# Attention layers of a hybrid backbone: order of the head preparation, token sums of squares, and the engine of the split differences

## Chip, cores, metric

One core of a Trainium2 chip runs the whole program. The metric is the device time of one execution in microseconds (us). A median is given with the runs it comes from; the profile is one execution with its own time.

## The reference, cut to what matters

Two layers work on 256 context and 256 latent tokens of width 1024. Each layer has a mixer and a sparse expert block.

```python
xr, ckv, kr, gk, gv, rg, cq, gq, mg = split_cols(h @ w_in, KV_SIZES + Q_SIZES)
kv = rms_norm(ckv, g_kv) @ w_ukv          # MLA: 8 heads, latent of 128
q  = rms_norm(cq, g_q) @ w_uq             # query latent of 256
t  = rms_norm(heads(gq or gk), g)         # GQA: per-head norm over 64
p  = softmax(q @ k.T * scale);  o = p @ v # latent tokens read 512 keys, context 256
out = sum(sigmoid(mg[k]) * (y[k] @ w_branch[k]) for k in (lru, mla, gqa)) @ w_out
```

Every `rms_norm` needs a sum of squares per token. In layer 0 all 512 tokens have queries (two query blocks per pair of heads); in layer 1 only the 256 latent ones (one block).

## The kernel before, in words

Activations stand with channels on partitions and tokens along the row. Large projections are made of three passes in the fast matmul format: weight and input are each split into a rounded part (hi) and the difference (lo), and hi\*hi, hi\*lo and lo\*hi are summed. `split` (L238) makes hi on ScalarE (L240) and lo either on VectorE (L242) or, when an engine is handed in, on GpSimd through `gtt` (L247). `wsplit` (L252) does it for a weight in tiles of 4 blocks of 128 rows; these tiles have 3 buffers (tag `sp`). `dense` (L262) is the three passes and `proj` (L409) a whole projection, which splits on VectorE. Matmuls in plain float32 count as two instructions in the trace.

`mixer` (L414) runs in this order. The recurrent input is projected and convolved. `lru(0)` and `lru(1)` (L488) work out the recurrence: matmuls, a chain of tanh and exp on ScalarE, one square root over a tile `lt` that has a single buffer, then products and scans on VectorE, with one product per direction and the sum `yr` on GpSimd. Between them the latents are projected: `ckv` (L556), the 32 columns `kr` (L565), `cq` (L572). Their squares are summed by a matmul with 32 columns of ones into rows (L561, L575), copied to SBUF (L563, L576) and turned to tokens by `tok_major` (L533), after which `rsqrt` (L153) runs one start and three rounds of three small dependent VectorE instructions. `gates` (L594) projects the gate of the recurrent branch, and `y0` (L611) is the product, split in hi and lo.

Then come MLA (branch 1) and GQA (branch 2) attention. Work that has nothing to do with the attention under way is laid between its steps: `fill` is a `Queue` (L73) of steps of the branch before. `merge` (L625) gives three steps for each of 8 column blocks j: `load_gate`/`gate0`, `split_gate`/`gate1`, `load_branch`/`branch`. Each first part (load and split) is issued one step before its matmuls. The modulation steps are put in the same queue. So the queue holds 37 steps for the MLA of layer 0 (24 merge, 13 modulation), 32 for its GQA, 25 and 24 in layer 1. TensorE keeps the program order from L814 on (`pin`); the other engines are ordered by the framework's scheduler.

`attend` (L728) walks over units (a pair of heads i and a query block). Per unit: `turn` (L710) turns a block of the softmax and ScalarE copies it out of the only `t` buffer, `scores` of the next unit, `values`. `fill.spread(gaps)` spreads what is left in the queue evenly over the gaps, 35 in layer 0 and 23 in layer 1; where there are fewer steps than gaps, some gaps get none, the first always. Before the attention, the steps that prepare the first pair of heads (`mla(0)`, L815: q_rope, turn_q, queries, keys, values; `gqa(0)`, L918: one) are issued with one fill step after each. The preparation of each later pair (`early`, L739 to L748) is issued during the last unit of the pair before, two steps after a turn, the rest at its end.

For GQA, `query` (L840) and `query_sums` (L849) are issued for four pairs, then the copy of the sums (L887), four `rope_in` (L888) with a fill step after every second, `tok_major` (L892), and `rsqrt` into `qrs` (L898), which every softmax of GQA multiplies (L682) before its exponential (L685).

Of the kernel before, what the change touches and what calls it, by code (L numbers as in the profile page):

```python
# [7 lines left out]
F32 = mybir.dt.float32  # L8
F32R = mybir.dt.float32r
BF16 = mybir.dt.bfloat16  # L10
I32 = mybir.dt.int32
AF = mybir.ActivationFunctionType
ALU = mybir.AluOpType
# [4 lines left out]
EPS = 1e-6  # L18
# [79 lines left out]
class Net:  # L98
# [307 lines left out]
            self.nc.vector.scalar_tensor_tensor(sc[:, :, r], sc[:, :, r], 1.0, g, op0=ALU.add, op1=ALU.mult)  # L406


    def proj(self, tag, w, c0, m, cs, hT, mark=None, xs=None):  # L409
        p = self.ps(tag)  # L410
        self.dense(p[:m, cs], self.wsplit(w, c0, 8, m), hT, xs or cs, mark=mark)
        return p

    def mixer(self, l, pb):  # L414
# [7 lines left out]
        t0 = lo // 128  # L422
# [17 lines left out]
        hT = []  # L440
# [89 lines left out]
            s.activation(q[:, cs], p[:, cs], AF.Square)  # L530
            return q

        def tok_major(rows, parts):  # L533

            pc = self.ps("t", (128, 4, 128))
            for t in range(4):
                n = parts(t)
                if n:
                    self.te.transpose(pc[:, t, :n], rows[:n, 128 * t:128 * t + 128], self.ident[:n, :n])
            return pc  # L540

        def rope_in(x, n, perm, cs, sn, eng):

# [11 lines left out]
        w = self.win(l, 512)  # L555
        p = self.proj("acc", w, 0, 128, A, hT, "ckv")  # L556
        ckv = self.gr("a", "ckv")
        q = sq_of(p, A)
        v.tensor_scalar(ckv, p, sm[:, SGKV:SGKV + 1], None, op0=ALU.mult)
        pa = self.ps("m")  # L560
        self.te.matmul(pa[0:32, :], self.ones32, q, start=True, stop=True)  # L561
        rows = self.sqp.tile([128, 512], F32, tag="rows", name="rows")
        v.tensor_copy(rows[:32, :], pa[:32, :])  # L563
        lru(0)
        p = self.proj("acc", w, 128, 32, A, hT)  # L565
        kr = self.gr("a", "kr")
        v.tensor_copy(kr[:32], p[:32])
        w = self.win(l, 1440)
        cq = [self.gl("a", "cq") for _ in range(2)]
        pa = self.ps("m")  # L570
        for i in range(2):
            p = self.proj("acc", w, 128 * i, 128, L, hT)  # L572
            q = sq_of(p, L)
            v.tensor_scalar(cq[i], p[:, L], self.gqs[l][:, i:i + 1], None, op0=ALU.mult)
            self.te.matmul(pa[32:64, L], self.ones32, q[:, L], start=i == 0, stop=i == 1)  # L575
        v.tensor_copy(rows[32:64, L], pa[32:64, L])  # L576
        rope_in(kr[:, 256:], 32, self.permM, self.cosM, self.sinM, v)
        pc = tok_major(rows, lambda t: 64 if t >= t0 else 32)
        ms = self.tiny([128, 4, 2], name="mms")
        v.memset(ms, 1.0)  # L580
        v.tensor_scalar(ms[:, :, 0:1], pc[:, :, 0:1], 1.0 / 128, EPS, op0=ALU.mult, op1=ALU.add)
        v.tensor_scalar(ms[:, t0:, 1:2], pc[:, t0:, 32:33], 1.0 / 256, EPS, op0=ALU.mult, op1=ALU.add)
        mrs = self.tiny([128, 4, 2], name="mrs")
        self.rsqrt(mrs, ms, [128, 4, 2])
        pb = self.ps("m")
# [8 lines left out]
        def gates(i2):  # L594
            w = self.win(l, 928 + 256 * i2)
            for i in (2 * i2, 2 * i2 + 1):
                p = self.proj("acc", w, 128 * (i % 2), 128, L, hT)
                a, x = self.gl("z", "ga"), self.gl("gt", "gx")
                s.activation(x, p[:, L], AF.Copy)
                s.activation(a, p[:, L], AF.Square, scale=0.044715 ** 0.5)  # L600
                v.scalar_tensor_tensor(a, a, 1.0, x, op0=ALU.add, op1=ALU.mult)
                s.activation(a, a, AF.Tanh, scale=0.7978845608028654)
                v.scalar_tensor_tensor(a, a, 1.0, x, op0=ALU.add, op1=ALU.mult)
                gel.append(a)
# [20 lines left out]
        def merge(b, j, y):  # L625

            c0 = 128 * (j % 2)

            def load_gate():
                if j % 2 == 0:  # L630
                    st["m"] = self.win(l, 2208 + 1024 * b + 128 * j)
                st[j, 0] = self.wsplit(st["m"][:, 0:4], c0, 4)
                st["m", j] = st["m"]

            def gate0():
                st["pm"] = self.ps("acc")
                self.dense(st["pm"][:, L], st.pop((j, 0)), hT[:4], L, last=False, mark=f"mg{b}.{j}")

            def split_gate():
                st[j, 1] = self.wsplit(st.pop(("m", j))[:, 4:8], c0, 4)  # L640

            def gate1():
                pm = st.pop("pm")
                self.dense(pm[:, L], st.pop((j, 1)), hT[4:], L, first=False)
                st["gt"] = gt = self.gl("gt", "gt")
                s.activation(gt, pm[:, L], AF.Tanh, scale=0.5)

            def load_branch():
                if j % 4 == 0:
                    st["b"] = self.wblock(ap["w_branch"][l, b, :, 512 * (j // 4):512 * (j // 4) + 512]  # L650
                                          .rearrange("(k p) c -> p k c", p=128), (4, 512))
                st[j, 2] = self.wsplit(st["b"], 128 * (j % 4), 4)

            def branch():
                gt, pp = st.pop("gt"), self.ps("acc")
                self.dense(pp[:, L], st.pop((j, 2)), y, Z)
                if b == 0:
                    zT[j] = self.gl("z", "zT")
                    v.scalar_tensor_tensor(zT[j], gt, 1.0, pp[:, L], op0=ALU.add, op1=ALU.mult)
                    return  # L660
                v.scalar_tensor_tensor(gt, gt, 1.0, pp[:, L], op0=ALU.add, op1=ALU.mult)  # L661
                self.gtt(zT[j], zT[j], gt, ALU.add)
                if b == 2:
                    hi, lw = self.gl("a", "zh", F32R), self.gl("a", "zl", F32R)
                    self.split(zT[j], hi, lw)
                    zs[j] = (hi, lw)

            return (load_gate, gate0), (split_gate, gate1), (load_branch, branch)
# [59 lines left out]
        def attend(units, early):  # L728
# [7 lines left out]
                    next(share)  # L736
            for n, u in enumerate(units):
                nxt = units[n + 1] if n + 1 < len(units) else None
                todo = list(early.pop(nxt.i, ())) if nxt and nxt.i != u.i else []  # L739
                for k, g_ in enumerate(u.groups):  # L740
                    u.turn(*g_)
                    if k < len(u.groups) - 1:
                        for f in todo[:2]:
                            f()
                        del todo[:2]
                        next(share)
                for f in todo:
                    f()  # L748
                if nxt:
                    nxt.scores(0)  # L750
                u.values()
                next(share)
                if nxt:
                    nxt.scores(1)
                next(share)
# [59 lines left out]
        for f in mla(0):  # L815
            f()
            fill()
        attend([Unit(i, st_, lambda i=i: [[(q[:96], k[:96])] for q, k in zip(QTs[i], KTs[i % 2])],
                     lambda c, hh, i=i: Vs[i][:, c, 64 * hh:64 * hh + 64], lambda t, hh: mrs[:, t, 1:2], y1)
                for i in range(4) for st_ in sts], {i: mla(i) for i in range(1, 4)})  # L820
# [9 lines left out]
        p = self.proj("acc", w, 128, 128, A, hT)  # L830
        gvT = self.gr("a", "gvT")
        s.activation(gvT, p, AF.Copy)
        pa = self.ps("m")
        self.te.matmul(pa[0:32, :], self.onesh, qk_, start=True, stop=True)
        rows = self.sqp.tile([128, 512], F32, tag="rows", name="rows")
        v.tensor_copy(rows[:32, :], pa[:32, :])
        gq, sqs = [], []
        pa = self.ps("o")

        def query(i):  # L840
            if i % 2 == 0:
# [5 lines left out]
            gq.append(x)  # L847

        def query_sums(i):  # L849
            self.te.matmul(pa[32 * i:32 * i + 32, L], self.onesh, sqs[i][:, L], start=True, stop=True)  # L850

        query(0)
        pc = tok_major(rows, lambda t: 32)
        ms = self.tiny([128, 4, 2], name="kms")
        v.tensor_scalar(ms, pc[:, :, 0:2], 1.0 / 64, EPS, op0=ALU.mult, op1=ALU.add)
        krs = self.tiny([128, 4, 2], name="krs")
# [26 lines left out]
        fill_branch(1, y1)  # L883
        fill(1)
        query_sums(3)
        rows = self.sqp.tile([128, 512], F32, tag="rows", name="rows")
        v.tensor_copy(rows[:, L], pa[:, L])  # L887
        for i in range(4):  # L888
            rope_in(gq[i][:, Tq - 256:], 128, self.permG, self.cosG, self.sinG, g)
            if i % 2 == 0:  # L890
                fill(1)
        pc = tok_major(rows, lambda t: 128 if t >= t0 else 0)  # L892
        ms = self.tiny([128, 4, 8], name="qms")
        v.tensor_scalar(ms[:, t0:].rearrange("p t (c r) -> p t c r", r=2),
                        pc[:, t0:, :].rearrange("p t (c r) -> p t c r", r=32)[:, :, :, 0:2],
                        1.0 / 64, EPS, op0=ALU.mult, op1=ALU.add)
        qrs = self.tiny([128, 4, 8], name="qrs")
        self.rsqrt(qrs[:, t0:], ms[:, t0:], [128, 4 - t0, 8])  # L898
        if l:
            for _ in self.fix:  # L900
                self.preload(l)
# [15 lines left out]

        for f in gqa(0):  # L918
            f()
            fill()  # L920
        attend([Unit(i, st_, lambda i=i: QK[i], lambda c, hh, i=i: gv[:, c, 64 * (i // 2):64 * (i // 2) + 64],
                     lambda t, hh, i=i: qrs[:, t, 2 * i + hh:2 * i + hh + 1], y2)
                for i in range(4) for st_ in sts], {i: gqa(i) for i in range(1, 4)})
# [850 lines left out]
```

## Time and profile before

| what | us |
|---|---|
| median of 3 runs (lowest, highest) | 1567.58 (1566.35, 1568.84) |
| the profiled execution, its own time | 1564.28 |
| span of its instructions | 1562.4 |
| TensorE matmul busy in the span | 1406.4 (90%) |
| VectorE, ScalarE, GpSimd busy | 845.8, 572.7, 183.5 |

The span runs: start and mixer of layer 0 to about 600, experts of layer 0 to 930, mixer of layer 1 to 1286, experts of layer 1 to the end. Busy shares are averages over these; what a mixer edit is worth is read from what TensorE waits for in the mixer's own stretches. The granted clock is given as a share of 2.4 GHz.

### The profile page before, as it was taken

The page shows a single profiled execution, that of the slowest core. Times are in us where ns is not written, and L with a number is a line of the kernel's source. Part 1 is how long each engine was busy: PE and PEld are TensorE (multiplying, and loading weights), DVE is VectorE, ACT ScalarE, POOL GpSimd, SP SyncE. Part 2 cuts the span into 40 slices and gives each one's busy share as a digit, 9 for nine tenths or more (in the row PEclk, how much of TensorE's full clock was granted, in tenths as well). Part 3 has the DMA queues.
Part 4 walks back from the last instruction along what each step waited for, and adds up shares of the span by engine and source line. Part 5 has one row for each costly group of instructions (what it writes and reads, how often), then busy time and mean ns, then how long its engine had stood idle before and what let it go on. Part 6 is the DMA issues. An engine that isn't in the chain of part 4 may idle for free. (4 is left out here: it accounts for less than half of the span.)

```text
span 1562.4 us, 19617 instructions
## 1 busy us (share of the span) xinstructions
PE 1406.4 (90%) x7313; PEld 877.1 (56%) x7313; DVE 845.8 (54%) x1963; ACT 572.7 (37%) x1122; POOL 183.5 (12%) x157
## 2 busy tenths in 40 slices
PE   6987899998989999699999969969979995999996
PEld 3645556666667776244444426656768992444433
DVE  4667545436654346745444456776476656444223
ACT  3455434433553342111111136635456551222212
POOL 0013200001101111200000010321010131000000
PEclk9999999999999999799999989979989997999998
DMA  9401323422313566799999823412232586999991
GB/s 357 160 28 53 135 108 108 145 71 81 135 55 133 197 263 259 270 420 419 414 409 392 330 99 108 162 54 73 90 108 82 189 325 240 419 419 419 419 417 50
DMA packets 61839, 336.56 MB, mean 215 GB/s; under 512 B 8864, under 2 KB 9376, under 8 KB 26272
## 3 DMA queue, kind: packets, MB, share of 16 engines
q1 hardware_dynamic: 55536, 324.20, 53.6%
q0 software_dynamic: 4608, 6.30, 1.2%
q10 hardware_dynamic: 1584, 4.64, 0.8%
q8 instruction: 62, 1.02, 0.3%
q14 instruction: 49, 0.40, 0.1%
HBM read 341.40 MB, written 4.19 MB: 221 GB/s over the span
## 5 line engine op out<-in xcount | busy, mean ns | idle before, releaser
L64 PE MATMUL ps_acc<-hTh,spl 128*128 128x512 f32 (+2 forms) x1280 | 373.2, 369 | 24.3 <-DVE spl L242 19.2
L64 PEld LDWEIGHTS ps_acc<-hTh,spl 128*128 128x128 f32 (+1 forms) x1280 | 232.4, 195 | 85.1 <-DVE spl L242 20.8
L242 DVE TENSOR_TENSOR spl<-wblk,spl 128x512 fp32r<-128x512 f32 (+1 forms) x245 | 179.7, 737 | 170.5 <-ACT spl L240 168.3
L64 PE MATMUL ps_acc<-hTl,spl 128*128 128x512 f32 (+1 forms) x640 | 228.9, 358 | 0.0
L64 PE MATMUL ps_s<-wblk,xg 128*64 128x512 f32 x936 | 216.1, 600 | 1.4 <-DMA wblk<-moe_w 1.4
L240 ACT ACTIVATE spl<-wblk 128x512 fp32r<-128x512 f32 x248 | 152.9, 622 | 167.0 <-PE ps_acc L64 148.3
L64 PEld LDWEIGHTS ps_acc<-hTl,spl 128*128 128x128 f32 x640 | 125.0, 195 | 21.9 <-issue 6.7
L64 PEld LDWEIGHTS ps_s<-wblk,xg 128*64 128x64 f32 x936 | 66.7, 138 | 121.6 <-issue 115.0
L1221 DVE SCALAR_TENSOR_TENSOR th<-th,ps_s 128x256 f32<-128x256 f32 x32 | 13.5, 422 | 204.7 <-ACT th L1220 204.6
L1013 DVE SCALAR_TENSOR_TENSOR xT<-ps_acc,modT,xT 128x256 f32<-128x256 f32 x216 | 93.3, 479 | 35.6 <-PE ps_acc L64 34.3
L64 PE MATMUL ps_acc<-yh,spl 128*128 128x512 f32 (+1 forms) x384 | 107.5, 352 | 0.0
L64 PE MATMUL ps_acc<-C,ob 128*128 128x512 f32 (+1 forms) x472 | 97.8, 352 | 7.5 <-DVE xT L1013 6.2
L1220 ACT ACTIVATE th<-ps_s 128x256 f32<-128x256 f32 x32 | 12.3, 384 | 218.8 <-PE ps_s L64 218.8
L64 PEld LDWEIGHTS ps_acc<-C,ob 128*128 128x128 f32 x472 | 71.0, 190 | 32.0 <-PE ps_acc L64 13.3
L64 PEld LDWEIGHTS ps_acc<-yh,spl 128*128 128x128 f32 x384 | 68.6, 193 | 11.2 <-issue 3.0
L1185 POOL DMA_INDIRECT xs<-hs,ri x32 | 34.4, 1074 | 330.8 <-PE ps_t L67 266.0
L681 DVE TENSOR_REDUCE nb<-ps_s 128x1 f32<-128x512 f32 (+1 forms) x96 | 55.5, 598 | 30.6 <-PE ps_s L64 30.2
L247 POOL TENSOR_TENSOR zT<-zT,gt 128x512 f32<-128x512 f32 (+1 forms) x32 | 39.7, 1239 | 257.3 <-DVE gt L661 249.4
L240 ACT ACTIVATE ob<-ps_o 128x512 fp32r<-128x512 f32 x30 | 17.9, 597 | 134.5 <-PE ps_o L64 134.5
L64 PE MATMUL ps_acc<-yl,spl 128*128 128x512 f32 (+1 forms) x192 | 65.6, 341 | 0.2 <-DVE yl L242 0.2
L64 PE MATMUL ps_acc<-zh,spl 128*128 128x512 f32 (+1 forms) x256 | 64.8, 340 | 0.0
L64 PE MATMUL ps_o<-wblk,heT 128*64 128x512 f32 x244 | 62.0, 605 | 0.0
(387 smaller groups left out, 2180.9 us busy)
## 6 DMA issues: line engine op xcount, KB each, us to landing
wblk<-moe_w SPq DMA_DIRECT2D x178, 1024.0 KB, 11.8
wblk<-w_in SPq DMA_DIRECT2D x40, 1024.0 KB, 4.9
wblk<-w_mod SPq DMA_DIRECT2D x37, 1024.0 KB, 4.9
wblk<-w_branch SPq DMA_DIRECT2D x12, 1024.0 KB, 5.1
wblk<-w_out SPq DMA_DIRECT2D x8, 1024.0 KB, 12.5
xT<-moe_w SPq DMA_DIRECT2D x7, 1024.0 KB, 20.1
misc<-moe_w SPq DMA_DIRECT2D x7, 1024.0 KB, 19.5
wblk<-w_mod SPq DMA_DIRECT2D x8, 512.0 KB, 7.6
```

The lines of the kernel that those rows point to most:

```text
L64: return self._put(self.tc.nc.tensor.matmul(*a, **k))
L240: self.nc.scalar.activation(hi, src, AF.Copy)
L242: self.nc.vector.tensor_tensor(lo, src, hi.bitcast(F32), op=ALU.subtract)
L247: self.nc.gpsimd.tensor_tensor(out, a, b, op=op)
L681: v.reduce_max(nb, pS[:, :n], axis=AX, negate=True)
L1013: self.nc.vector.scalar_tensor_tensor(x, p[:, plo + 256 * s:plo + 256 * s + 256], G[:, j, r:r + 1], x, op0=ALU.mult, op1=ALU.add)
L1185: g.indirect_dma_start(xs, None, self.hs[l], bass.IndirectOffsetOnAxis(ap=ri[:, 0:1], axis=0), bounds_check=T - 1, oob_is_err=False)
L1220: s.activation(th, ph[:, 0, :], AF.Tanh, scale=0.5)
L1221: v.scalar_tensor_tensor(th, th, 1.0, ph[:, 0, :], op0=ALU.add, op1=ALU.mult)
```

## The change

Sums of squares are made by matmuls with the squares as weights and ones as one or two moving columns, so that they land on tokens directly (`tok_sums`). The 32 columns `kr` are projected with hi and lo side by side as one 64-column weight. `cq`, `gates`, `load_gate` and `load_branch` hand GpSimd to the split. The later pairs of heads are prepared one step after each turn, from the first unit of the pair before. Two fill steps more follow the whole of `mla(0)`, two instead of one follow `gqa(0)`, one follows each GQA rope, and the query `rsqrt` stands ahead of the ropes.

```diff
-    def proj(self, tag, w, c0, m, cs, hT, mark=None, xs=None):
+    def proj(self, tag, w, c0, m, cs, hT, mark=None, xs=None, eng=None):
...
-        self.dense(p[:m, cs], self.wsplit(w, c0, 8, m), hT, xs or cs, mark=mark)
+        self.dense(p[:m, cs], self.wsplit(w, c0, 8, m, eng), hT, xs or cs, mark=mark)
...
-        def tok_major(rows, parts):
...
+        def tok_sums(pc, col, qs, ones, ts):
+
+            n = ones.shape[-1]
+            for t in ts:
+                for i, q in enumerate(qs):
+                    self.te.matmul(pc[:, t, col:col + n], q[:, 128 * t:128 * t + 128], ones, start=i == 0,
+                                   stop=i == len(qs) - 1)
...
-        p = self.proj("acc", w, 128, 32, A, hT)
+
+        p = self.ps("acc")
+        for k0 in range(0, 8, 4):
...
+            self.split(w[:, k0:k0 + 4, 128:160], t[:, :, 0:32], t[:, :, 32:64], g)
...
+                low = lambda: self.te.matmul(p[:32], t[:, k, 0:32], xl, start=False, stop=False, skip_group_check=True)
...
+                self.te.matmul(p[:64], t[:, k], xh, start=k0 + k == 0, stop=k0 + k == 7, skip_group_check=True)
...
-        v.tensor_copy(kr[:32], p[:32])
+        krl = self.sqp.tile([128, 512], F32, tag="sq", name="krl")
+        s.activation(krl[:32], p[32:64], AF.Copy)
+        v.tensor_tensor(kr[:32], p[:32], krl[:32], op=ALU.add)
...
-            p = self.proj("acc", w, 128 * i, 128, L, hT)
-            q = sq_of(p, L)
+            p = self.proj("acc", w, 128 * i, 128, L, hT, eng=g)
+            qs.append(sq_of(p, L))
...
+        tok_sums(pc, 0, [qkv], self.ones32[:, :1], range(4))
+        tok_sums(pc, 1, qs, self.ones32[:, :1], range(t0, 4))
...
-                p = self.proj("acc", w, 128 * (i % 2), 128, L, hT)
+                p = self.proj("acc", w, 128 * (i % 2), 128, L, hT, eng=g)
...
-                st[j, 0] = self.wsplit(st["m"][:, 0:4], c0, 4)
+                st[j, 0] = self.wsplit(st["m"][:, 0:4], c0, 4, eng=g)
...
-                st[j, 2] = self.wsplit(st["b"], 128 * (j % 4), 4)
+                st[j, 2] = self.wsplit(st["b"], 128 * (j % 4), 4, eng=g)
...
-                todo = list(early.pop(nxt.i, ())) if nxt and nxt.i != u.i else []
+                if not n or units[n - 1].i != u.i:
+                    todo = list(early.get(u.i + 1, ()))
                 for k, g_ in enumerate(u.groups):
                     u.turn(*g_)
+                    if todo:
+                        todo.pop(0)()
                     if k < len(u.groups) - 1:
-                        for f in todo[:2]:
-                            f()
-                        del todo[:2]
                         next(share)
-                for f in todo:
-                    f()
+                while nxt and nxt.i != u.i and todo:
+                    todo.pop(0)()
...
         for f in mla(0):
             f()
             fill()
+        fill(2)
...
-            self.te.matmul(pa[32 * i:32 * i + 32, L], self.onesh, sqs[i][:, L], start=True, stop=True)
+            tok_sums(pq, 2 * i, [sqs[i]], self.onesh[:, :2], range(t0, 4))
...
-        rows = self.sqp.tile([128, 512], F32, tag="rows", name="rows")
-        v.tensor_copy(rows[:, L], pa[:, L])
+        ms = self.tiny([128, 4, 8], name="qms")
+        v.tensor_scalar(ms[:, t0:], pq[:, t0:, 0:8], 1.0 / 64, EPS, op0=ALU.mult, op1=ALU.add)
+        qrs = self.tiny([128, 4, 8], name="qrs")
+        self.rsqrt(qrs[:, t0:], ms[:, t0:], [128, 4 - t0, 8])
         for i in range(4):
             rope_in(gq[i][:, Tq - 256:], 128, self.permG, self.cosG, self.sinG, g)
-            if i % 2 == 0:
-                fill(1)
...
+            fill(1)
...
         for f in gqa(0):
             f()
-            fill()
+            fill(2)
```

## Rows read from the trace of the kernel before

**Rows 1.** Busy time by stretch; columns as in the second line.
```profile
core 0: us, PE busy (x) PEld busy (x) DVE busy (x) ACT busy (x) POOL busy (x), PEclk, DMA share, GB/s
310.00:361.00 51.00, 49.81 (x222) 34.94 (x220) 21.83 (x46) 19.04 (x32) 7.43 (x7) 1.00 0.25 83
361.00:475.00 114.00, 101.54 (x548) 75.39 (x547) 67.46 (x190) 55.50 (x123) 9.53 (x7) 0.97 0.25 84
962.00:979.00 17.00, 17.00 (x69) 8.80 (x68) 6.34 (x10) 15.91 (x22) 0.00 (x0) 1.00 0.14 55
962.00:1046.00 84.00, 66.81 (x346) 43.64 (x344) 60.52 (x107) 49.44 (x81) 23.54 (x17) 0.90 0.31 112
1161.00:1221.00 60.00, 51.21 (x376) 44.88 (x377) 42.81 (x105) 33.51 (x72) 4.88 (x6) 0.91 0.22 80
1221.00:1262.00 41.00, 40.92 (x338) 40.47 (x337) 27.69 (x50) 22.80 (x49) 9.18 (x9) 1.00 0.57 210
```

**Rows 2.** Waits of PE, 73 to 560 us (layer 0): total us, times, longest.
```profile
PE ps_s L64 <- ACT P L685: 7.1, 5, 4.2
PE ps_acc L64 <- DVE spl L242: 6.8, 1, 6.8
PE ps_s L64 <- ACT lt L501: 5.6, 1, 5.6
PE ps_m L64 <- ACT QT L802: 4.4, 3, 1.8
PE ps_t L67 <- ACT PT L718: 3.9, 4, 1.4
PE ps_m L64 <- DVE qr L783: 2.6, 2, 1.8
PE ps_m L64 <- DVE ra L547: 2.3, 2, 1.2
```

**Rows 3.** Waits of PE, 940 to 1262 us (layer 1).
```profile
PE ps_acc L64 <- DVE spl L242: 12.4, 3, 8.9
PE ps_s L64 <- ACT P L685: 9.0, 2, 7.2
PE ps_t L67 <- ACT PT L718: 3.8, 3, 1.7
PE ps_m L64 <- ACT QT L802: 3.0, 3, 1.3
PE ps_m L64 <- DVE ra L547: 1.6, 2, 1.1
```

**Rows 4.** SP's queue at the end of mixer 0 (timeline).
```profile
600.30 17.11 SPq L145 DMA_DIRECT2D wblk<-moe_w  x9
```

**Rows 5.** PE timeline: a sum with columns of ones; two token sums.
```profile
963.59 1.04 PE L64 MATMUL ps_m<-sqn,cst 128*32 128x512 f32 x2
...
1286.71 0.36 PE L64 MATMUL ps_m<-cst,rows 128*128 128x1 f32 x2
1286.93 0.36 PE L64 MATMUL ps_m<-cst,sq 128*128 128x1 f32 x2
```

**Rows 6.** VectorE timeline, layer 1: first and last of the eleven instructions of the query root.
```profile
1158.42 0.17 DVE L894 TENSOR_SCALAR qms<-ps_t 128x16 f32<-128x16 f32 x1
...
1165.22 0.18 DVE L160 SCALAR_TENSOR_TENSOR qrs<-nt,qrs 128x16 f32<-128x16 f32 x1
```

**Rows 7.** PE timeline, layer 1: the first two scores of GQA.
```profile
1159.45 0.39 PE L64 MATMUL ps_s<-gkl,qs 128*128 128x512 f32 x1
1167.00 0.79 PE L64 MATMUL ps_s<-gkh,qs 128*128 128x512 f32 x1 [7.15 <-ACT P L685]
```

**Rows 8.** Groups by line and shape: a split difference on VectorE, one on GpSimd.
```profile
L242 DVE TENSOR_TENSOR spl<-wblk,spl 128x512 fp32r<-128x512 f32 x241 | 178.5, 745 | 170.2 <-ACT spl L240 168.0
L247 POOL TENSOR_TENSOR hTl<-hf,hTh 128x512 fp32r<-128x512 f32 x8 | 10.3, 1291 | 60.0 <-ACT hTh L240 60.0
```

**Rows 9.** Timeline, layer 1: VectorE before and beside a GpSimd product, and that product.
```profile
1015.48 0.69 DVE L511 SCALAR_TENSOR_TENSOR lt<-la,lt 128x512 f32<-128x512 f32 x1
1016.68 1.75 DVE L511 SCALAR_TENSOR_TENSOR lt<-la,lt 128x512 f32<-128x512 f32 x1
...
1016.34 1.55 POOL L247 TENSOR_TENSOR lg<-lg,lt 128x512 f32<-128x512 f32 x1 [12.26 <-DVE lt L511]
```

More of the change, by code (lines that the diff above doesn't have):

```diff
@@ L531, in sq_of @@
             return q
-        def tok_major(rows, parts):
[L535 to L540, printed above, removed]
+        def tok_sums(pc, col, qs, ones, ts):
[4 more added lines that the diff above has]
+                                   stop=i == len(qs) - 1)
         def rope_in(x, n, perm, cs, sn, eng):
@@ L557, in mixer @@
         ckv = self.gr("a", "ckv")
-        q = sq_of(p, A)
+        qkv = sq_of(p, A)
         v.tensor_scalar(ckv, p, sm[:, SGKV:SGKV + 1], None, op0=ALU.mult)
-        pa = self.ps("m")
-        self.te.matmul(pa[0:32, :], self.ones32, q, start=True, stop=True)
-        rows = self.sqp.tile([128, 512], F32, tag="rows", name="rows")
-        v.tensor_copy(rows[:32, :], pa[:32, :])
         lru(0)
-        p = self.proj("acc", w, 128, 32, A, hT)
+        p = self.ps("acc")
+        for k0 in range(0, 8, 4):
+            t = self.mx.tile([128, 2, 4, 128], F32R, tag="sp", name="spl")[:, 0, 0:2].rearrange("p a (b c) -> p (a b) c", c=64)
+            self.split(w[:, k0:k0 + 4, 128:160], t[:, :, 0:32], t[:, :, 32:64], g)
+            for k in range(4):
+                xh, xl = hT[k0 + k]
+                low = lambda: self.te.matmul(p[:32], t[:, k, 0:32], xl, start=False, stop=False, skip_group_check=True)
+                if k0 + k:
+                    low()
+                self.te.matmul(p[:64], t[:, k], xh, start=k0 + k == 0, stop=k0 + k == 7, skip_group_check=True)
+                if not k0 + k:
+                    low()
         kr = self.gr("a", "kr")
-        v.tensor_copy(kr[:32], p[:32])
+        krl = self.sqp.tile([128, 512], F32, tag="sq", name="krl")
+        s.activation(krl[:32], p[32:64], AF.Copy)
+        v.tensor_tensor(kr[:32], p[:32], krl[:32], op=ALU.add)
         w = self.win(l, 1440)
         cq = [self.gl("a", "cq") for _ in range(2)]
-        pa = self.ps("m")
+        qs = []
         for i in range(2):
-            p = self.proj("acc", w, 128 * i, 128, L, hT)
-            q = sq_of(p, L)
+            p = self.proj("acc", w, 128 * i, 128, L, hT, eng=g)
+            qs.append(sq_of(p, L))
             v.tensor_scalar(cq[i], p[:, L], self.gqs[l][:, i:i + 1], None, op0=ALU.mult)
-            self.te.matmul(pa[32:64, L], self.ones32, q[:, L], start=i == 0, stop=i == 1)
-        v.tensor_copy(rows[32:64, L], pa[32:64, L])
+        pc = self.ps("t", (128, 4, 128))
+        tok_sums(pc, 0, [qkv], self.ones32[:, :1], range(4))
+        tok_sums(pc, 1, qs, self.ones32[:, :1], range(t0, 4))
         rope_in(kr[:, 256:], 32, self.permM, self.cosM, self.sinM, v)
-        pc = tok_major(rows, lambda t: 64 if t >= t0 else 32)
         ms = self.tiny([128, 4, 2], name="mms")
@@ L581, in mixer @@
         v.tensor_scalar(ms[:, :, 0:1], pc[:, :, 0:1], 1.0 / 128, EPS, op0=ALU.mult, op1=ALU.add)
-        v.tensor_scalar(ms[:, t0:, 1:2], pc[:, t0:, 32:33], 1.0 / 256, EPS, op0=ALU.mult, op1=ALU.add)
+        v.tensor_scalar(ms[:, t0:, 1:2], pc[:, t0:, 1:2], 1.0 / 256, EPS, op0=ALU.mult, op1=ALU.add)
         mrs = self.tiny([128, 4, 2], name="mrs")
@@ L832, in mixer @@
         s.activation(gvT, p, AF.Copy)
[L833 to L836, printed above, removed]
+        pc = self.ps("t", (128, 4, 128))
+        tok_sums(pc, 0, [qk_], self.onesh[:, :2], range(4))
         gq, sqs = [], []
-        pa = self.ps("o")
+        pq = self.ps("o", (128, 4, 128))
         def query(i):
@@ L849, in query_sums @@
         def query_sums(i):
-            self.te.matmul(pa[32 * i:32 * i + 32, L], self.onesh, sqs[i][:, L], start=True, stop=True)
+            tok_sums(pq, 2 * i, [sqs[i]], self.onesh[:, :2], range(t0, 4))
         query(0)
-        pc = tok_major(rows, lambda t: 32)
         ms = self.tiny([128, 4, 2], name="kms")
@@ L885, in mixer @@
         query_sums(3)
-        rows = self.sqp.tile([128, 512], F32, tag="rows", name="rows")
-        v.tensor_copy(rows[:, L], pa[:, L])
+        ms = self.tiny([128, 4, 8], name="qms")
+        v.tensor_scalar(ms[:, t0:], pq[:, t0:, 0:8], 1.0 / 64, EPS, op0=ALU.mult, op1=ALU.add)
+        qrs = self.tiny([128, 4, 8], name="qrs")
+        self.rsqrt(qrs[:, t0:], ms[:, t0:], [128, 4 - t0, 8])
         for i in range(4):
             rope_in(gq[i][:, Tq - 256:], 128, self.permG, self.cosG, self.sinG, g)
-            if i % 2 == 0:
-                fill(1)
[L892 to L898, printed above, removed]
+            fill(1)
         if l:
```

## Prediction, made before the changed kernel was run

> **What bounds the kernel now.** I read the busy time by stretch first, then TensorE's waits in the two mixers, then the timelines around the longest waits. Outside the mixers nothing is edited. The expert weights of layer 0 begin to load when its mixer ends, at 600.3 [rows 4], so I take a microsecond won in a mixer as one won at the end.
>
> Inside the mixers TensorE is the bound in some stretches: between 310 and 361 it is busy 49.8 of 51 us, in the last branch of layer 1 40.9 of 41 [rows 1]. There only less matmul work helps. Elsewhere it stands: 12.5 of 114 us in the GQA of layer 0, 8.8 of 60 in that of layer 1, 17.2 of 84 in the preparation of layer 1, at a lower clock (0.97, 0.91, 0.90) [rows 1]. What ends these waits differs. In the preparation it is VectorE's split differences (6.8 us in layer 0, 12.4 in layer 1) and the single `lt` buffer (5.6) [rows 2, 3]. At a change of heads it is the copy of the new queries (4.4 and 3.0). At the start of GQA it is the first softmax: 4.2 and 7.2 us, the longest of their rows [rows 2, 3].
>
> **The change part by part**, in us of the end; minus is a gain.
>
> *Token sums.* A sum with ones columns takes about 1.0 us for 512 tokens [rows 5], some 0.55 for 256 as I scale it; a token sum takes 0.22, from one start to the next [rows 5]. I put a set of four row transposes at 0.4, between twice a token sum and a ones sum. Layer 0 drops 3 sums and 1 set for MLA (3.4) for 12 token sums (2.6), and 5 sums and 2 sets for GQA (5.8) for 20 (4.4). Layer 1 drops 1 long, 2 short and 0.6 for MLA (2.7) for 8 (1.8), and 1 long, 4 short and 0.7 for GQA (3.9) for 12 (2.6). Together −4.5, all of it in TensorE's order. The four VectorE copies of rows go too; VectorE idles beside them, so they count nothing, and at the worst nothing is lost.
>
> *`kr` with hi and lo side by side.* Eight matmuls fewer per layer, 0.22 each (49.8 us over 222) [rows 1]: 1.8 per layer. I count nothing: from 962 to 979 ScalarE is busy 15.9 of 17 us with the recurrence, and the next matmuls need what it makes [rows 1]. The added ScalarE copy and VectorE sum work on 32 rows; they lengthen that chain by one short step at most. Ends −3.7 and +1.5. Without the cover the gain appears.
>
> *The query root ahead of the ropes.* In layer 1 its eleven dependent instructions take from 1158.4 to 1165.4 [rows 6], although each lasts under 0.2 us, because ropes, head splits and reductions were scheduled among them. The first softmax cannot begin before, and TensorE stands for 7.15 us behind its score buffers [rows 7]. With the root started before the ropes this wait should fall to that of a softmax which starts undisturbed. The other wait of the same row in layer 1, at the start of MLA, is 9.0 − 7.2 = 1.8 [rows 3]. So −5.4 there and, by the same 1.8, −2.4 in layer 0. The fill step now behind every rope covers the waits for `ra`, 1.2 and 0.5 [rows 2, 3]: −1.7. The granted clock of these stretches, 0.97 and 0.91, lies between the levels of 2.4 and 1.2 GHz; a mean of 0.91 over 60 us means some 11 at the lower, of which up to 8.8 were idle. I take −1.5 for matmuls that ran slowly after the waits. Together −11. Ends: −14 if the wait goes wholly, −3 if the scheduler still lays other work among the root. The weight loads on SP keep their order; each is only asked for earlier.
>
> *Heads prepared in steps.* The waits at head changes are 4.4 + 3.0 for the query copies and about 0.8 of `qr` (2.6 − 1.8) [rows 2, 3]. After the change a turn and mostly a fill step lie between two preparation steps, which is enough for a copy. I count −6. Ends −8.2 and 0. Late next would be the copy of the turned softmax (the `t` buffer).
>
> *Fill steps moved to the front.* Total fill is the same, so it is missed later. MLA keeps 30 instead of 32 steps for 35 gaps in layer 0 and 18 instead of 20 for 23 in layer 1; GQA 25 instead of 28, and 17 instead of 20. Gaps without a step grow from 3 + 7 + 3 + 3 = 16 to 5 + 10 + 5 + 6 = 26. The waits for the turned softmax, 3.9 + 3.8 in 7 times [rows 2, 3], are what such a gap costs: 1.1 where it bites, 0.5 over all 16. Ten more cost 5; in MLA preparation steps stand in for some: +4. Ends 0 and +11. The two fills behind `mla(0)` cover no wait of the trace, since the first gap behind the first scores stays empty: nothing.
>
> *Splits on GpSimd.* Per layer 4 tiles of `cq`, 8 of `gates` and two of three merge splits, 48: 120 in all. Each costs GpSimd 1.29 us and frees VectorE of 0.745 [rows 8]. The gain is that a split no longer queues behind the recurrence on VectorE. The loss shows in the timeline: the same VectorE instruction takes 0.69 us alone and 1.75 when GpSimd has begun a product just before; it waits until that one ends at 1017.9 [rows 9]. So while a split runs on GpSimd, such an instruction of VectorE with two inputs in SBUF gets nothing done, and a moved split takes 1.29 from VectorE's backlog instead of 0.745. In the preparation the waits at stake are 6.8 + 12.4 + 5.6 = 24.8 [rows 2, 3]. But behind them stands the product `y0`, which ends the same VectorE chain, and behind that the GpSimd copies and products of the recurrence, which now queue with the splits. I take a quarter, −6; ends −24.8 and +13 (24 splits there, 0.55 each). In the last branch of layer 1 a block j lasts 36 matmuls of 0.12 us, 4.4, on a TensorE without a gap; GpSimd's share grows from 1.0 to 1.0 + 2 × 1.29 = 3.6, in one queue whose sums wait for VectorE [rows 1, 8]. A late split stops TensorE at once. I take +2; ends 0 and +6. In the other fills a step has attention work beside it; nothing.
>
> The Trainium skill, page "SBUF — State Buffer", section "Who interferes with whom", says that GpSimd shares VectorE's second port pair under an exclusive lock for the whole instruction. By that rule the moves free nothing for VectorE and the sum would be worse by what the second rival below gives; the trace agrees with it [rows 9].
>
> The sum: −4.5 − 11 − 6 + 4 − 6 + 2 = −21.5. Against the profiled execution, 1564.3, that is 1542.8. The median of the runs is 3.3 higher; I forecast on the median: **1546**.
>
> **Rivals.**
> 1. *The waits only move* (1556). The empty gaps bite fully, 10 × 1.1 = +11 instead of +4, and head changes keep half their wait, −3 instead of −6: −11.5. For it: the `t` wait already shows in both mixers. Against it: most gaps still have a step. The change would then not do what it says between the heads.
> 2. *Slower: GpSimd's splits hold VectorE up* (1576). Place: preparation and merges. Price: 120 × 0.55 = 66 us of extra VectorE hold; with all of the preparation (13) and a quarter of the merges (13) on TensorE's path, +26 in place of −6 and +2: −17.5 + 26 = +8.5. It decides once over a quarter of the 66 us (17.5) reaches TensorE. For it: VectorE is busy 60.5 of 84 us in the preparation of layer 1 and GpSimd 23.5 already [rows 1]. Against it: in the two GQA stretches VectorE is idle 41% and 29% of the time [rows 1], and fill hides what it loses.
> 3. *The preparation opens up* (1534). The splits of `cq`, of the last gates and of the first merges find GpSimd free while VectorE works off the recurrence; most of the 24.8 goes, −18 instead of −6: −33.5. For it: GpSimd is idle 60 of these 84 us. Against it: `y0`.
> 4. *Nothing arrives* (1567). The expert streams absorb the gain. Against it: rows 4.
>
> **How the numbers follow.** Forecast 0.46, rival 1 0.22, rival 2 0.10, rival 3 0.18, rival 4 0.04. Faster by over 0.2% (3.1 us, about what a measurement of this kernel can tell) is the forecast with rivals 1 and 3, 0.86; within it 0.04; slower 0.10. The forecast alone would lie within 1540 to 1552. The range takes in rivals 1 and 3 and the spread of their unknown costs, 1529 to 1563, and leaves out 2 and 4 and tails.
>
> **What would show it.** Right: the wait for the first GQA softmax under 2.5 us in both layers; no wait for query copies over 0.5; more waits for the `t` copy; the ones sums gone. Wrong: long waits for GpSimd's splits in the preparation or in 41 us of the last branch, or VectorE busy time that has not fallen though half its splits left; or mixers that end earlier by more than the whole does.

## The result, and the profile after

The change made the kernel **slower**: 1576.43 us (median of 4 runs) beside 1566.96 of before (4 runs), ratio 1.0063, 95% interval 1.0048 to 1.0077. The forecast was 1546 with a range to 1563; both miss. The price of the second rival, 1576, was the one that came.

The busy times of the kernel after show the exchange. Before, VectorE was busy 845.8 us in 1963 instructions and GpSimd 183.5 in 157.

```profile
span 1574.5 us, 19706 instructions
PE 1406.5 (89%) x7347; PEld 889.3 (56%) x7347; DVE 792.9 (50%) x1831; ACT 575.2 (37%) x1124; POOL 339.1 (22%) x281
```

GpSimd took on 156 us and VectorE lost only 53. The groups by line and shape say why: the 120 large splits that left VectorE would have freed 120 × 0.745 = 89 us [rows 8], but what stayed there got longer (`kr`'s four small splits moved too). First the kernel after:

```profile
L247 POOL TENSOR_TENSOR spl<-wblk,spl 128x512 fp32r<-128x512 f32 x123 | 168.2, 1371 | 505.1 <-ACT spl L240 486.0 <-PE ps_s L64 17.9 <-POOL KT L250 0.6
L242 DVE TENSOR_TENSOR spl<-wblk,spl 128x512 fp32r<-128x512 f32 x121 | 93.2, 772 | 138.8 <-ACT spl L240 138.0
L517 DVE TENSOR_TENSOR_SCAN lg<-la,lg 128x512 f32<-128x512 f32 x8 | 12.8, 1604 | 0.0
L519 DVE TENSOR_TENSOR_SCAN lg<-la,lg 128x256 f32<-128x256 f32 x8 | 11.7, 1461 | 6.1 <-POOL lg L247 6.1
```

The two scans before took 1.20 and 0.67 us (ns, shortest/median/longest):

```profile
L517 DVE TENSOR_TENSOR_SCAN lg<-la,lg x8: 1192/1203/1211, 92.6 to 1021.3; 128x512 f32<-128x512 f32 x8
L519 DVE TENSOR_TENSOR_SCAN lg<-la,lg x8: 657/669/678, 93.7 to 1025.5; 128x256 f32<-128x256 f32 x8
```

TensorE's waits after, first 73 to 565 us (layer 0), then 944 to 1273 (layer 1), answer to [rows 2] and [rows 3]; smaller ones are left out (...):

```profile
PE ps_acc L64 <- DVE kr L576: 12.9, 1, 12.9
PE ps_m L64 <- DVE qr L792: 12.7, 1, 12.7
PE ps_s L64 <- ACT P L694: 7.2, 5, 2.3
PE ps_t L67 <- ACT PT L727: 4.7, 6, 0.8
...
PE ps_m L64 <- ACT QT L811: 0.8, 1, 0.8
...
PE ps_m L64 <- DVE qr L792: 7.2, 1, 7.2
PE ps_acc L64 <- DVE cq L583: 7.0, 1, 7.0
PE ps_t L67 <- ACT PT L727: 6.8, 8, 2.1
PE ps_m L64 <- DVE KT L819: 4.2, 3, 2.0
PE ps_s L64 <- ACT P L694: 3.8, 3, 2.1
PE ps_acc L64 <- POOL spl L247: 3.7, 6, 1.2
```

The attention did in part as foreseen: the longest softmax waits fell from 4.2 and 7.2 to 2.3 and 2.1, those for the query copies from 4.4 and 3.0 to 0.8 and none. But the softmax waits of layer 0 together stayed (7.1 before, 7.2 after), and those for the key copies (`KT`) in layer 1 grew from 1.7 to 4.2. The loss is in the preparation. Its waits name `kr`, `qr` and `cq`, all late outputs of VectorE; only 3.7 us name a split made on GpSimd. The name of a wait is not yet its price, as the first two experiments show. The preparation of layer 1, from the scaling of `ckv` to the first matmul on `ckv`, before and then after (columns as in [rows 1]):

```profile
963.50:1035.70 72.20, 58.21 (x313) 38.14 (x313) 55.49 (x97) 46.35 (x76) 20.50 (x15) 0.91 0.31 111
```
```profile
968.10:1050.40 82.30, 60.83 (x312) 41.91 (x311) 50.06 (x80) 47.58 (x77) 44.19 (x31) 0.85 0.28 100
```

It lasts 10.1 us longer for as many matmuls (312 and 313): TensorE is idle 7.5 us more, and its matmuls take 2.6 us more at a granted clock of 0.85 instead of 0.91. VectorE has 17 instructions fewer and is relieved of only 5.4 us. In layer 0 the first matmul on `ckv` comes at 172.3 instead of 163.4; attention there gives back four of these 8.9 us, and the first matmul of `w_out` comes at 557.7 instead of 552.8.

### The profile page after: what moved, and what is told of

Read it like the earlier page. It is cut to its first block, busy times and chain, and to the rows that moved or that the text cites. A ratio compares the mean times of both kernels' runs of the same rounds, so it can differ in the third digit from the quotient of the medians.

```text
span 1574.5 us, 19706 instructions
## 1 busy us (share of the span) xinstructions
PE 1406.5 (89%) x7347; PEld 889.3 (56%) x7347; DVE 792.9 (50%) x1831; ACT 575.2 (37%) x1124; POOL 339.1 (22%) x281
## 5 line engine op out<-in xcount | busy, mean ns | idle before, releaser
L247 POOL TENSOR_TENSOR spl<-wblk,spl 128x512 fp32r<-128x512 f32 (+1 forms) x127 | 170.0, 1343 | 536.4 <-ACT spl L240 517.2
L242 DVE TENSOR_TENSOR spl<-wblk,spl 128x512 fp32r<-128x512 f32 x121 | 93.2, 772 | 138.8 <-ACT spl L240 138.0
L1222 DVE SCALAR_TENSOR_TENSOR th<-th,ps_s 128x256 f32<-128x256 f32 x32 | 13.5, 422 | 206.5 <-ACT th L1221 206.4
L67 PE MATMUL ps_t<-cst,P 128*128 128x128 f32 x320 | 51.0, 283 | 14.6 <-ACT PT L727 11.5
```

What stands on the lines that cost most here:

```text
L67: return self._put(self.tc.nc.tensor.transpose(*a))
L242: self.nc.vector.tensor_tensor(lo, src, hi.bitcast(F32), op=ALU.subtract)
L247: self.nc.gpsimd.tensor_tensor(out, a, b, op=op)
L1222: v.scalar_tensor_tensor(th, th, 1.0, ph[:, 0, :], op0=ALU.add, op1=ALU.mult)
```

## Experiments

All were timed against the kernel before on the same chip in five rounds; 0.1% is 1.6 us. Each stands as its ratio to before with the 95% interval. By the half-widths of two such intervals, added in squares, a difference of two ratios is uncertain by 0.2 to 0.3%, 3 to 4 us. Theory A was that the preparation's splits on GpSimd hold VectorE up; B that `kr` does it; C the merge splits; D the moved fills and steps.

**The preparation's splits on VectorE again** (`cq`, gates and the four small ones of `kr`), the rest as after:
```diff
-            p = self.proj("acc", w, 128 * i, 128, L, hT, eng=g)
+            p = self.proj("acc", w, 128 * i, 128, L, hT)
...
```


> The splits of cq, gates and kr are made on VectorE again; the merge splits stay on GpSimd. Theory A (the loss is the preparation's splits on GpSimd, which hold VectorE up): the 15 us that the preparations lost come back, 1576.4 - 15 = about 1561, range 1555 to 1566, and the products and scans of the recurrence last as long as before (scan of 512 columns 1.2 us). Theory B (the loss is kr's late VectorE sum, which keeps an accumulator busy): no change, 1573 to 1578. Theory C (the loss is the merge splits in the fill steps): no change, 1573 to 1578.

Measured 1.0005 (0.9991 to 1.0019): 0.58%, 9 us come back of the 15 that A expected. Theory A, at the upper end of its range.

**The merge splits on VectorE again** (`load_gate`, `load_branch` without `eng=g`):

> The merge splits are made on VectorE again; the preparation's stay on GpSimd. Theory A: little, 1570 to 1577, since GpSimd and VectorE both have idle time in attention. Theory C: most of the loss comes back, 1555 to 1566. Theory B: 1573 to 1578.

1.0052 (1.0032 to 1.0072), 1.7 us better than after, with overlapping intervals. C falls as the main cause. Here the wait for `qr` in layer 0, 12.7 us after, is down to 1.7, while with the preparation's splits on VectorE it is still 11.8. So the move that removes this long wait brings the smaller gain: with `qr` in time, TensorE stands there 7.9 us for a VectorE split, for which it did not stand in the kernel after.

**All splits of the change on VectorE:**

> No split of the change on GpSimd; token sums, early query root, stepped heads, moved fills and kr side by side stay. Theory A: the other terms of the forecast stand (-17.5 from 1567), about 1549, range 1545 to 1560. Theory B: kr's late sum is still there and still holds TensorE, 1572 to 1578. Theory D (the moved fills and steps cost more than the attention terms win): 1568 or more.

0.9986 (0.9971 to 1.0000). A is right about the splits, but its 1549 is missed by far: without any split moved, the rest of the change wins 2 us instead of 17.5. So two steps of the forecast had failed. Between the kernel with only the preparation's splits on VectorE (1.0005) and this one the merges are worth 0.19%, 3 us, with intervals that touch. In the profiles the preparation of layer 1 is 2.9 us longer with the merges on GpSimd (77.6 beside 74.7); three of their splits run in it.

**`kr` as before**, in the kernel after and, next, without the splits:
```diff
-        for k0 in range(0, 8, 4):
...
-        v.tensor_tensor(kr[:32], p[:32], krl[:32], op=ALU.add)
+        p = self.proj("acc", w, 128, 32, A, hT)
+        kr = self.gr("a", "kr")
+        v.tensor_copy(kr[:32], p[:32])
```


> kr is projected as before (32 rows, hi and lo apart, one VectorE copy, its split on VectorE), the rest as after. Theory B: TensorE's wait for the kr sum (12.9 us in layer 0) goes, and so do most of the 9.5 us lost, 1562 to 1568. Theory A: that wait only changes its name, 1573 to 1578, at best 3 us for the four splits that leave GpSimd.

> As no split of the change on GpSimd, and kr projected as before (hi and lo apart, one VectorE copy). Theory B2 (kr's late VectorE sum is what the preparation still loses): 4 to 6 us faster than with kr side by side, 1557 to 1560. Rival (the later token sums lose it, kr is even): within 2 us, 1561 to 1566.

1.0083 (1.0062 to 1.0103) and 0.9973 (0.9960 to 0.9985): 0.2% worse in the one, 0.13% better in the other, both within the intervals. B falls as the cause of the loss: with the old copy TensorE still waits 10.7 us for it in layer 0, and with `kr` side by side but the preparation's splits on VectorE that wait is 0.3. A small price of the new `kr` without moved splits is not excluded: the preparation of layer 1 is then 74.7 us in one profile and 72.1 with the old `kr`.

**One part alone**, in the kernel before: `eng=g` for the splits of `cq` and of the gates, nothing else.

> The kernel before with one part of the change alone: the splits of cq and of the gates on GpSimd. Theory A: slower by what moving them back has won, about 10 us, 1573 to 1579, with scans of 512 columns at about 2.3 in place of 1.2 us. Rival (the splits hurt only together with the new kr and token sums): within 3 us of before, 1564 to 1569.

1.0102 (1.0082 to 1.0122): 24 moved splits cost 16 us by themselves, more than theory A's range. The scans of 512 columns average 1.47 us, not 2.3; single ones reach 2.3.

**Queue or hold?** GpSimd also makes products and sums of the recurrence, and these queue behind the splits. The control moves them (16 instructions) to VectorE; the next kernel has in addition the splits of `cq` and gates on GpSimd.
```diff
-                    self.gtt(h, h, t, ALU.mult)
+                    v.tensor_tensor(h, h, t, op=ALU.mult)
...
-                    self.gtt(y, G_[i, 0][:, L], h[:, L], ALU.add)
+                    v.tensor_tensor(y, G_[i, 0][:, L], h[:, L], op=ALU.add)
```


> The kernel before, with the recurrence's products of one direction and its sums (16 instructions) on VectorE instead of GpSimd: the control for the next kernel. Some 16 instructions of 0.7 to 0.4 us more for VectorE, in the chain that TensorE waits for: 0 to 8 us slower than before, 1565 to 1573.

> The kernel before with the splits of cq and gates on GpSimd (1.0102 of before), and the recurrence's products and sums on VectorE, so that nothing of the recurrence queues behind a split on GpSimd. Theory Q (the loss is the queue: products of the recurrence stand behind splits on GpSimd): the loss against the control falls from 16 us to 4 or less. Theory L (the loss is VectorE, held while a split runs on GpSimd): 10 us or more slower than the control, with products and scans of VectorE still at twice their length.

The control is 0.9958 (0.9941 to 0.9974), faster, which I had not expected; with the splits moved 1.0044 (1.0030 to 1.0059). The loss against the control is 0.86%, 13.5 us, though nothing of the recurrence queues on GpSimd: theory L, VectorE held up while a split runs on GpSimd. TensorE's waits that name a split from GpSimd are 1.2 us in the whole profile. The timeline of that kernel shows the hold (three GpSimd splits merged in one row, 993.20 to 998.07):

```profile
993.20 4.87 POOL L247 TENSOR_TENSOR spl<-wblk,spl 128x512 fp32r<-128x512 f32 x3 [5.68 <-PE ps_s L64]
993.69 0.42 DVE L576 COPY rows<-ps_m 32x256 f32<-32x256 f32 x1
994.14 1.20 DVE L513 TENSOR_TENSOR lg<-lg,lt 128x512 f32<-128x512 f32 x1
995.37 1.64 DVE L519 TENSOR_TENSOR_SCAN lg<-la,lg 128x256 f32<-128x256 f32 x1
997.04 0.41 DVE L547 TENSOR_TENSOR ra<-ps_m,misc 32x256 f32<-32x256 f32 x1
997.38 1.24 DVE L521 TENSOR_TENSOR_SCAN lg<-la,lg 128x256 f32<-128x256 f32 x1
...
117.71 1.30 POOL L247 TENSOR_TENSOR spl<-wblk,spl 128x512 fp32r<-128x512 f32 x1 [3.39 <-ACT spl L240]
117.80 1.23 DVE L160 SCALAR_TENSOR_TENSOR mrs<-nt,mrs 128x8 f32<-128x8 f32 x1
```

Products and scans that read two tiles of SBUF last 1.7 to 2.5 times as long (L513, L519 and L521 average 0.68, 0.67 and 0.74 in the control). The two that read PSUM (`ps_m`) keep their 0.42 and 0.41 in the same five microseconds. In layer 0 even an instruction of 8 columns, 0.17 us elsewhere, lasts 1.23, until the split ends (117.71 + 1.30). The Trainium skill, page "SBUF — State Buffer", section "Who interferes with whom", says that a VectorE instruction with two inputs in SBUF contends with a GpSimd instruction that reads SBUF, and one with at most one such input, outside the two-port modes, does not; these rows agree with both halves.

**A hold that nobody waits for.** The control, every split on VectorE, with each split of `cq` and gates repeated on GpSimd (a shadow) into weights that are dead by then:
```diff
+            if eng is not None:
+                self.gtt(w[:, k0:k0 + 4, c0:c0 + m], w[:, k0:k0 + 4, c0:c0 + m], hi.bitcast(F32), ALU.subtract)
```


> The control with the recurrence on VectorE (0.996 of before), every split on VectorE, and behind each of the 24 splits of cq and gates the same subtraction once more on GpSimd, written over weights that nothing reads any more: no computing instruction waits for it. Theory L (VectorE held while GpSimd subtracts): most of the 14 us loss against the control without any split arriving later, so 8 to 16 us over it, 1564 to 1573. Theory W (the split arrives late, by GpSimd's slower subtraction and its queue): within 3 us of the control, 1554 to 1560.

1.0055 (1.0037 to 1.0073), 0.97% or 15 us over the control. GpSimd makes no split of a weight that a matmul waits for, and the loss is there: theory L. In the preparation of layer 1 the same 105 VectorE instructions take 60.4 instead of 52.8 us, and the stretch is 8.0 us longer (the control's line stands under "The hold shows twice"):

```profile
968.80:1045.10 76.30, 59.77 (x314) 38.94 (x314) 60.43 (x105) 47.02 (x77) 29.21 (x21) 0.91 0.28 104
```

A shadow also keeps its split's tile and its weight buffer occupied. In this stretch that cost little: ScalarE waits 0.4 us for shadows, and its longest wait for a weight load is 6.8 us here as in the control. In layer 0 the first matmul on `ckv` comes 4.3 us later, of which 0.8 are left at the first matmul of `w_out`. Then 4.1 us more pass up to the preparation of layer 1. The edit reaches further than the 24 splits: three splits of layer 1's recurrent input, which GpSimd makes in every other kernel here, become VectorE splits with a shadow too, and beside these shadows (930.23 to 934.90) TensorE waits 8.1 us for the norm's `rs` instead of 5.2. So by these profiles some 4 of the 15 us are not the price of the 24 shadows.

> The control with the recurrence on VectorE, with the splits of the gates alone (16 of 24) on GpSimd. If the loss goes by the number of splits: two thirds of 14, 9 us over the control, about 1566. If it sits where cq is projected, among the recurrence of the first heads: under 5 us, 1557 to 1561. If it sits at the gates: 11 us or more, 1568 to 1572.

With the gates alone 1.0009 (0.9996 to 1.0022), 0.51% or 8 us over the control, beside 13.5 for all 24: within the errors the loss goes by the number of splits, 0.5 and 0.56 us each.

**The attention edits alone**, the preparation as before and no split moved: first with all of them, then with the old places of the fill steps, then also with the old head preparation. The two steps back:
```diff
-        fill(2)
         attend([Unit(i, st_, lambda i=i: [[(q[:96], k[:96])]
...
-            fill(1)
+            if i % 2 == 0:
+                fill(1)
...
-            fill(2)
+            fill()
...
-                    if todo:
-                        todo.pop(0)()
+                        for f in todo[:2]:
+                            f()
+                        del todo[:2]
```


> The preparation as in the kernel before (kr, token sums of MLA, all splits on VectorE, merges too); of the change only the GQA token sums, the early query root, the stepped heads and the moved fills. Theory A2 (with the splits back on VectorE the preparation still loses some 3 us per layer through its reordered kr and token sums, and attention wins about 8): the 6 us come back, 1567 - 8 = about 1558, range 1555 to 1561. Rival (the preparation's 3 us are only a shift that attention takes up anyway): as with no split of the change on GpSimd, 1562 to 1566.

> As the attention edits alone, with the fill steps where they were before (one behind each first head's step, one behind every second rope). Theory: the moved fills cost about as much later as they cover, within 2 us of the attention edits alone. Rival D (the moved fills give back what the root and the steps win, through the turned-softmax waits of 5.8 in place of 3.8 us and the softmax waits): 3 to 6 us faster than the attention edits alone.

> Of the change only the GQA token sums and the early query root; heads prepared and fill steps placed as before, all splits on VectorE. Theory: the root and the sums bring 6 to 8 us of layer 1 and little in layer 0, so 1558 to 1561, and the stepped heads the 2 to 4 us that then lack to the version with steps and the old fills (0.994 of before). Rival: the steps bring nothing, within 1.5 us of that version, 1554 to 1557.

0.9981 (0.9968 to 0.9994), 0.9942 (0.9927 to 0.9958) and 0.9959 (0.9944 to 0.9975). The first is within the error of the kernel with all of the change but the splits (0.9986): the new order of the preparation is even, the 6 us that I expected back were not there. The second is rival D: the moved fills cost 6 us. The third: sums and root win 6.4 us, the steps 2.7, which the intervals don't separate from nothing. In layer 1 the steps remove the 3.0 us of waits for query copies, but those for key copies grow from 1.7 to 3.3.

**Moved fills in layer 0 only** (each of the three edits under `if full`):

> The attention edits alone, with the moved fills in layer 0 only. Theory (moving a fill pays in layer 0, where 28 to 32 steps meet 35 gaps, and costs 1.5 us each in layer 1, where 20 meet 23): 1549 to 1553, faster than both the version with all fills moved (0.998) and that with none (0.994). Rival (the two profiles differ by chance, the moved fills cost in both layers): 1555 to 1560.

0.9912 (0.9891 to 0.9934), 11 us faster than with all fills moved. In layer 1 the moved steps are a loss; in layer 0 they win some 4.7 us, with intervals that touch. Two stretches of layer 1 show part of the loss, from the last MLA score to the first GQA score and from there to the last; first with all fills moved, then in layer 0 only:

```profile
1106.30:1160.50 54.20, 51.19 (x377) 46.84 (x376) 34.56 (x81) 29.72 (x62) 6.72 (x7) 1.00 0.36 130
1160.50:1207.40 46.90, 38.98 (x273) 32.21 (x272) 32.75 (x81) 26.30 (x58) 4.98 (x5) 0.96 0.21 76
```
```profile
1099.10:1148.50 49.40, 47.90 (x352) 43.79 (x351) 30.85 (x74) 27.47 (x57) 6.29 (x7) 1.00 0.30 107
1148.50:1196.70 48.20, 42.03 (x297) 36.24 (x296) 36.96 (x88) 28.50 (x62) 3.78 (x5) 0.93 0.29 110
```

25 matmuls more ahead of the scores lengthen the first stretch by 4.8; 24 fewer shorten the second by 1.3 only, where TensorE is now idle 7.9 instead of 6.2 us. That is 3.5 of the 11 us. Most of the rest stands ahead of them, from the first matmul on `ckv` to the last MLA score: 71.8 beside 65.9 us. Of these 5.9 some 3 are spread between executions, since the kernel with the old fills, the same in layer 1, takes 69.1.

**What won, together:** the attention edits, fills moved in layer 0, no split moved, and the recurrence on VectorE.

> What won, together: GQA token sums, early query root, stepped heads, moved fills in layer 0 only (0.991 of before), no split of the change on GpSimd, and the recurrence's products and sums on VectorE (0.996 of before). If both gains add: 0.987, about 1543; if the second is only a shift that the first takes up: 0.990 to 0.991, 1549 to 1551.

0.9851 (0.9831 to 0.9871), 1541.9 us: both gains add, and it beats both kernels.

## Why the prediction was wrong, step by step

From the kernels above, each number the difference of two ratios times 1566:

| term | forecast | measured | from |
|---|---|---|---|
| GQA sums and early root | −13.7 | −6.4 | sums and root alone |
| heads in steps | −6 | −2.7 (not separated from 0) | old fills, with and without steps |
| moved fills | +4 | +6.1 | attention edits, new and old fills |
| MLA sums and `kr` | −1.8 | +0.8 (not separated) | no split moved, beside attention alone |
| merge splits | +2 | +3.0 (intervals touch) | no split moved, beside preparation's on VectorE |
| preparation's splits | −6 | +9.1 | preparation's on VectorE, beside after |
| sum | −21.5 | +9.9 | |

**The step that failed first** is "the gain is that a split no longer queues behind the recurrence on VectorE ... I take a quarter, −6". It makes 15 of the 31 us between forecast and result. The premise before it was right: [rows 9] showed the hold. What was wrong is to set a gain against it. The waits of 24.8 us that I wanted to shorten were for VectorE's chain, in which the moved splits were a small part (12 × 0.745 = 8.9 of 55.5 us in layer 1); a split on GpSimd holds that chain up, whatever queue it stands in.

The price of 0.55 per split lies among what the runs give, 0.4 to 0.7 us (9.1, 13.5 and 16 us for 24, 8 for 16), but that is luck. It was to be VectorE's net loss, and VectorE's busy time in the preparation of layer 1 did not grow: with 12 splits moved it fell from 52.8 to 51.7 us. By the shadows the hold is 7.6 / 12 = 0.63 per split, a little less than what a moved split frees. What costs is that the hold falls on the recurrence, which TensorE waits for; this is how I read the waits, and no run measures it apart.

The second rival had this mechanism, and hit the time by two errors that cancel, which is luck too: of its 26 us only 9 + 3 = 12 reached TensorE (the preparation 9 for its 13, the merges 3 for 13), less than the 17.5 from which it should decide (a quarter of the 66 us is 16.5); but the rest of the change won 2 us instead of 17.5. That the merges cost so little because VectorE had room beside them [rows 1] is argued, not shown.

**The hold shows twice**, as idle time and as slower matmuls. The control and the kernel with the splits moved, in the preparation of layer 1:

```profile
963.80:1032.10 68.30, 56.33 (x314) 36.93 (x314) 52.80 (x105) 46.36 (x76) 9.90 (x8) 0.93 0.32 117
```
```profile
968.20:1046.50 78.30, 63.95 (x313) 42.88 (x313) 51.73 (x93) 46.92 (x76) 28.05 (x20) 0.85 0.28 102
```

10.0 us longer, of which 7.6 are as many matmuls lasting longer at a granted clock of 0.85 instead of 0.93, and 2.4 more idle. The shares are those of this execution, which was 4.8 us slower than its kernel's median: before and after it was 2.6 and 7.5, control and shadows 3.4 (at 0.91) and 4.6. I counted the clock as −1.5 beside the root and not at all here.

**The second step** is the root, −11. In layer 1 it nearly came: the stretch from the last MLA score to `w_out` fell from 150.5 to 144.0 us with sums and root alone, −6.5 beside my −5.4 − 1.3 − 0.5 = −7.2. The first softmax wait went from 7.15 [rows 7] to 3.4, not to 1.8. In layer 0 the same stretch kept its 265.0 (265.1): the first wait shrank from 4.2 to 2.6, the wait for `ra` grew from 1.2 to 2.2, and the last branch took 94.2 instead of 92.5 at 0.98 instead of 1.00 of the clock. I had added up waits as if each was worth its length.

**Moved fills** kept my sum (+6 for +4, within the end of +11), but not its place: about −5 in layer 0 and +11 in layer 1, where 17 steps met 23 gaps. The waits for the turned softmax grew as foreseen, 3.8 to 6.8 in layer 1. **Heads in steps**: the waits for query copies went, but 7.4 us of waits were worth some 2.7, with later key copies in their place. **Token sums of MLA and `kr`**: nothing that shows (my token sums add up to −4.4, not −4.5). **"The waits only move"** was right that head changes keep about half of their price and that moved fills bite in layer 1, but it kept my −6 for the preparation, and with it missed. **"Nothing arrives" and "the preparation opens up"** are ruled out by the result itself.

Of my marks for wrong, "VectorE busy time that has not fallen" came in part, with 53 of 89 us; "long waits for GpSimd's splits" did not come, since TensorE waits for what the hold makes late, not for the splits. The marks for right came almost all (one wait of 0.8 for a query copy was over 0.5), in a slower kernel: they looked at the attention alone.

## What to carry to other kernels

In this kernel an instruction moved from VectorE to GpSimd did not help where VectorE worked through products and scans with two inputs in SBUF: beside them it took back nearly all the VectorE time that it freed, and it delayed what TensorE waited for. So ask what VectorE does in that stretch, not how busy it is overall. Do the reverse test too: taking GpSimd's work out of such a stretch paid here although VectorE had more to do. And fill work that was moved ahead paid only in the layer where enough of it was left for the gaps behind.

## What was not expected of the hardware

Moving the recurrence's 16 products and sums to VectorE made the kernel 0.42% faster. In the preparation of layer 1 VectorE then makes 105 instructions in 52.8 us, and made 97 in 55.5 before, while GpSimd falls from 20.5 to 9.9 us. The sixteen products of L511, which stood beside GpSimd's, average 0.70 us instead of 1.14: the same hold, taken away.

The hold goes both ways: beside a VectorE that works without a break, a GpSimd split lasted longer too. In the kernel after, one of layer 1 took 3.95 us instead of 1.29. It began while VectorE was in a run of five instructions with two inputs in SBUF, from 983.82 to 987.43, which kept their lengths, and ended 1.08 us after that run. That VectorE is the cause is read from this place; no run tests it.

```profile
984.56 3.95 POOL L247 TENSOR_TENSOR spl<-wblk,spl 128x512 fp32r<-128x512 f32 x1 [5.44 <-ACT spl L240]
983.82 1.27 DVE L511 SCALAR_TENSOR_TENSOR lt<-la,lt 128x512 f32<-128x512 f32 x2
985.03 0.67 DVE L515 TENSOR_TENSOR lg<-lg,lt 128x512 f32<-128x512 f32 x1
985.63 0.67 DVE L511 SCALAR_TENSOR_TENSOR lt<-la,lt 128x512 f32<-128x512 f32 x1
986.23 1.20 DVE L517 TENSOR_TENSOR_SCAN lg<-la,lg 128x512 f32<-128x512 f32 x1
```
